# Up projections of a SwiGLU block as seven block products, with the down projections summed in PSUM

## Chip, cores, metric

One NeuronCore of a Trainium2 chip. The metric is the device time of one execution in microseconds, the median of three runs. Five engines run side by side: TensorE (PE; its weight loads are listed as PEld), VectorE (DVE), ScalarE (ACT), GpSimd (POOL) and SyncE (SP), which here issues every transfer.

## What is computed

Two layers of a hybrid block on 512 latent tokens (stream x) and 256 context tokens (stream ctx), width 1024. Layer 1 (the last) runs its second half for x alone. The change touches the tail of each layer:

```python
D_MODEL, SEQ, CTX_LEN, D_FF = 1024, 512, 256, 2816
def residual_tail(x, mix, g1, sh2, sc2, g2, w_out, ln1g, ln1b, w1, w3, w2, ln2g, ln2b):
    x = layer_norm(DEEPNORM_ALPHA * x + g1 * (mix @ w_out), ln1g, ln1b)
    h = x * (1.0 + sc2) + sh2
    ffn = (jax.nn.silu(h @ w1) * (h @ w3)) @ w2
    return layer_norm(DEEPNORM_ALPHA * x + g2 * ffn, ln2g, ln2b)
```

The modulation vectors (sh, sc, g) of a layer are a product of the conditioning with w_mod, 1024 x 6144.

## The kernel before

Everything is fp32. Each operand of a product is split into a rounded part hi and a rest lo (`split`, L168 the cast on ACT, L169 the difference, mostly on DVE), and `mm3` (L172 to L174) adds lo*hi, hi*lo and hi*hi in PSUM, so every product is three matmuls. Weights come through `wload`: a transfer into one of 4 staging buffers (`S4`, L186), then a split into one of 5 pairs (`W8`). Activations lie in 22 buffers `U` and in scratch buffers `FT` (10 in the feed-forward part). PSUM has 4 single banks (`PS`) and 2 double ones (`PD`).

`wout_ffn` does the output projection and the feed-forward part. The 2816 features are 22 tiles of 128. The projection of x runs in two halves of tokens (`wout_mm`), and while the second half is projected, the first is normalised (`res_ln1`, `ln1`, whose last step is L947), transposed and split (`to_hT`, L348, L350). POOL makes the scaled residual of each token tile (`residual`, L954, L955). Then come chunks of 2 feature tiles, the last of 4. For each tile, `upk` multiplies the 8 k-tiles of w1 and of w3 with the activations of a stream (512 tokens of x, 256 of ctx), takes silu on ACT (L1077), the product on DVE (L1078) and splits the result. Then each token tile's part of the down projection is summed over the chunk in a `PD`, multiplied by the gate on DVE (L1154) and added to the residual on POOL (L1155). `ffn_last` does the last chunk, tile by tile, with the LayerNorm behind it; the very last tile goes in quarters of 256 columns.

The program is written in this order, and a scheduler with its own times then orders each engine's queue. Weights are requested in the order of a list (`add`, `getw` with a look-ahead). In layer 0, `fill(2)` puts two steps of the next layer's modulation (`mods`, loads L258, matmuls L272) behind each feature tile: four loads of 512 KB in the same staging buffers.

```python
for k in range(KD):
    mm3(ps[:, :n], w[0][:, k], w[1][:, k], st.hT[k][:, 0, sl], st.hT[k][:, 1, sl], k == 0, k == KD - 1)
```

## Time and profile before

| | us |
|---|---|
| three runs, median (lowest to highest) | 1692.19 (1691.33 to 1692.58) |
| profiled execution, span | 1690.5 |
| PE busy | 1612.5 (95%) |
| DVE, ACT, POOL busy | 919.2, 628.0, 499.4 |
| transfers | 190.82 MB, mean 113 GB/s |

The span runs from the first to the last instruction of one profiled execution; what lies around it (start and end) is in the runs' times and not in the span, 1.7 us by the median. Engine times are sums of instructions, and engines overlap. A matmul's record includes its pipeline, so records of neighbours overlap. The granted clock of PE is given as a share of 2.4 GHz.

### The profile page before, as it was taken

Reading aid. Unit: us, or ns where it says so; the run is one execution under the profiler, and the core shown is the slowest. Engines: PE = TensorE matmul, PEld = TensorE weight load, DVE = VectorE, ACT = ScalarE, POOL = GpSimd, SP = SyncE. Lnnn points to the kernel's source line nnn. Section 1 sums busy time; section 2 is a strip of 40 time slices with the busy share of each in tenths; the row PEclk is TensorE's granted clock in tenths of the full one; section 3 lists DMA queues with packets and bytes.
Section 4 is the critical chain, followed back from the end, with each engine's and each line's share of the span. In section 5 each row is a group of like instructions: output and inputs, shape, how many; then the busy total and the mean of one; then the engine's idle time right before and its main releaser. Section 6 shows DMA issues by size and latency. Waiting matters only on the chain.

```text
span 1690.5 us, 22196 instructions
## 1 busy us (share of the span) xinstructions
PE 1612.5 (95%) x8745; PEld 1339.2 (79%) x8745; DVE 919.2 (54%) x1229; ACT 628.0 (37%) x1113; POOL 499.4 (30%) x412
## 2 busy tenths in 40 slices
PE   6999889999999999999999997989999899999997
PEld 3857778897888887888888876879988788888886
DVE  1434676868843434432444358577859554445455
ACT  2521666875411212121221235457954322212221
POOL 0213011323533133421433015342323432233223
PEclk9999999999999999999999998999999899999999
DMA  9576113135425534453321214411145133222321
GB/s 322 176 223 191 40 39 135 63 108 177 128 64 162 159 103 143 127 167 111 114 64 49 63 51 135 131 57 38 38 161 184 55 97 115 88 87 88 112 99 50
DMA packets 148236, 190.82 MB, mean 113 GB/s; under 512 B 7290, under 2 KB 108268, under 8 KB 148132
## 3 DMA queue, kind: packets, MB, share of 16 engines
q1 hardware_dynamic: 148132, 189.41, 35.2%
q8 instruction: 69, 1.13, 0.3%
q14 instruction: 35, 0.29, 0.1%
HBM read 184.10 MB, written 5.28 MB: 112 GB/s over the span
## 4 chain that ended last, share of the span: by engine, by line
PE 82%; DVE 8%; DMA 3%; ACT 3%; issue 3%; POOL 1%; SPq 0%; POOLq 0%; DVEq 0%; ACTq 0%
PE ps L172 14%; PE ps L174 14%; PE ps L173 14%; PE pd L172 10%; PE pd L173 10%; PE pd L174 10%; PE ps L272 3%; PE ps L719 3%; PE ps L703 2%; DVE u L169 2%; DVE w L169 2%; DMA u<-in_w_mod_dram 1%; ACT u L168 1%; ACT w L168 1%; DMA i<-in_ctx_dram 1%
## 5 line engine op out<-in xcount | busy, mean ns | idle before, releaser
L173 PE MATMUL ps<-u,w 128*128 128x512 f32 (+1 forms) x1216 | 424.5, 349 | 6.7 <-DVE u L169 6.7
L172 PE MATMUL ps<-u,w 128*128 128x512 f32 (+1 forms) x1216 | 423.8, 349 | 1.3 <-DVE modT L298 1.0
L174 PE MATMUL ps<-u,w 128*128 128x512 f32 (+1 forms) x1216 | 423.9, 349 | 0.0
L169 DVE TENSOR_TENSOR w<-s,w 128x1024 fp32r<-128x1024 f32 (+4 forms) x225 | 311.1, 1390 | 193.9 <-ACT w L168 193.0
L168 ACT CAST w<-s 128x1024 fp32r<-128x1024 f32 (+4 forms) x225 | 227.7, 1025 | 506.4 <-PE pd L174 203.4
L1155 POOL TENSOR_TENSOR f<-f,f 128x1024 f32<-128x1024 f32 x90 | 241.4, 2691 | 525.8 <-DVE f L1154 525.8
L172 PE MATMUL pd<-w,u 128*128 128x512 f32 (+5 forms) x824 | 313.2, 380 | 10.5 <-DVE u L169 8.6
L173 PE MATMUL pd<-w,u 128*128 128x512 f32 (+5 forms) x824 | 309.8, 376 | 2.3 <-DVE w L169 2.3
L174 PE MATMUL pd<-w,u 128*128 128x512 f32 (+5 forms) x824 | 307.8, 374 | 0.0
L173 PEld LDWEIGHTS ps<-u,w 128*128 128x128 f32 x1216 | 231.2, 190 | 41.4 <-DVE u L169 7.9
L172 PEld LDWEIGHTS ps<-u,w 128*128 128x128 f32 x1216 | 230.6, 190 | 40.0 <-DVE u L169 3.6
L174 PEld LDWEIGHTS ps<-u,w 128*128 128x128 f32 x1216 | 231.0, 190 | 35.2 <-issue 4.2
L1154 DVE TENSOR_TENSOR f<-pd,f 128x1024 f32<-128x1024 f32 x90 | 110.0, 1222 | 192.3 <-PE pd L174 192.3
L172 PEld LDWEIGHTS pd<-w,u 128*128 128x128 f32 x824 | 156.4, 190 | 52.3 <-DVE u L169 10.8
L173 PEld LDWEIGHTS pd<-w,u 128*128 128x128 f32 x824 | 156.5, 190 | 32.0 <-issue 3.4
L174 PEld LDWEIGHTS pd<-w,u 128*128 128x128 f32 x824 | 156.5, 190 | 29.1 <-issue 1.7
L168 ACT CAST u<-y 128x512 fp32r<-128x512 f32 (+1 forms) x222 | 109.6, 516 | 187.5 <-DVE y L1078 174.0
L169 POOL TENSOR_TENSOR u<-y,u 128x512 fp32r<-128x512 f32 (+1 forms) x60 | 79.0, 1323 | 226.6 <-ACT u L168 204.3
L169 DVE TENSOR_TENSOR u<-y,u 128x256 fp32r<-128x256 f32 (+1 forms) x162 | 107.4, 681 | 50.4 <-ACT u L168 49.7
L1078 DVE TENSOR_TENSOR y<-ps,y 128x512 f32<-128x512 f32 (+1 forms) x70 | 40.2, 574 | 163.4 <-PE ps L174 163.4
L1077 ACT ACTIVATE y<-ps 128x512 f32<-128x512 f32 (+1 forms) x70 | 35.2, 503 | 162.0 <-PE ps L174 161.9
L355 POOL TENSOR_SCALAR st<-st 128x1 f32<-128x1 f32 x30 | 8.3, 277 | 250.6 <-DVE st L1025 125.9
(217 smaller groups left out, 1811.7 us busy)
## 6 DMA issues: line engine op xcount, KB each, us to landing
s<-in_w_ffn_dram SPq DMA_DIRECT2D x132, 512.0 KB
s<-in_w_mod_dram SPq DMA_DIRECT2D x80, 512.0 KB
s<-in_w_out_dram SPq DMA_DIRECT2D x50, 512.0 KB
u<-in_w_mod_dram SPq DMA_DIRECT2D x16, 512.0 KB
s<-in_w_in_dram SPq DMA_DIRECT2D x16, 512.0 KB
s<-in_w_in_dram SPq DMA_DIRECT2D x12, 416.0 KB
...
```

What stands on the lines that cost most here:

```text
L168: A_.copy(out=hi, in_=src)
L169: (eng or V_).tensor_tensor(out=lo, in0=src, in1=f(hi), op=ALU.subtract)
L172: T_.matmul(ps, lhsT=ll, rhs=rh, start=start, stop=False)
L173: T_.matmul(ps, lhsT=lh, rhs=rl, start=False, stop=False)
L174: T_.matmul(ps, lhsT=lh, rhs=rh, start=False, stop=stop)
L272: T_.matmul(ps[32 * j:32 * j + 32, :n], lhsT=sst[:, k, :], rhs=ws[j // 2][:, (j % 2) * n:(j % 2 + 1) * n], start=(k == 0), stop=(k == KD - ...
L703: T_.transpose(pt[:, o:o + P], es[t2][:, k * P:(k + 1) * P], ident)
L719: T_.matmul(av[:, 0:256], lhsT=vt[k][:, h, :], rhs=pts[k // 2][:, a, (k % 2) * 256:(k % 2 + 1) * 256], start=(k == 0 and a == 1), stop=(k ...
L1077: A_.activation(out=y, in_=p1[:, :n], func=AF.Silu)
L1078: V_.tensor_tensor(out=y, in0=p3[:, :n], in1=y, op=ALU.mult)
L1154: V_.tensor_tensor(out=tt, in0=pd.rearrange("p a b -> p (a b)"), in1=gb[st.s], op=ALU.mult)
L1155: G_.tensor_tensor(out=yacc[(st.s, t)], in0=yacc[(st.s, t)], in1=tt, op=ALU.add)
```

## The change

The activations are cut into 2 x 2 blocks: k-tiles 0 to 3 and 4 to 7, and two halves of the tokens, N = 384 each in layer 0 (two x tiles and one ctx tile) and 256 in layer 1. The weights of a feature tile are a 2 x 2 block too: w1 over w3, k-tiles 0 to 3 beside 4 to 7. Of the 22 tiles the first 2 (`NCONV`) are multiplied as before, by token halves; the other 20 take seven block products (Winograd's form) where the plain way has eight. For that

- `up_forms` loads w1 and w3 of a tile into staging and leaves them there until POOL has made four differences and sums of them (L1073, L1074, L1077, L1078, 128x512 each) and ACT and DVE have split seven blocks into three pairs `W8` and one `FT`;
- once a layer, `T1` to `T4`, differences of activation blocks (L1179; 12 on DVE, 4 on POOL), are made and split, 16 pieces;
- `prod` is 4 k-tiles x 3 matmuls (L1186); `finish` completes a tile one iteration later; sums of products in PSUM and SBUF are on DVE (L1218, L1233, L1194), the products with silu on POOL (L1195, L1196);
- the result of each tile is stored to DRAM (`yd`), and the residuals too (`rd`, L1134).

The down projections follow after all 22 tiles: one pass over all features per group of token tiles, two passes of three tiles in layer 0 (w2 is loaded and split twice), one of four in layer 1, summed in PSUM; activations are loaded back and split (`feat`). The gate is multiplied once (in layer 1 into all of w2, L189 of before). `FT` has 14 buffers.

```diff
-        scoped[0] = tc.tile_pool(name=nm(kind), bufs={"inp": 10, "att": 1, "ffn": 10}[kind], reuse_waits="tile")
+        scoped[0] = tc.tile_pool(name=nm(kind), bufs={"inp": 10, "att": 1, "ffn": 14}[kind], reuse_waits="tile")
...
+    NCONV, NLAST = 2, 4
...
+    def up_forms(l, ft):
+        s1, s3 = getw(("1", l, ft), 2), getw(("3", l, ft), 2)
+        lo, hi = slice(0, 512), slice(512, 1024)
+        with tc.high_priority(offset=WOFF):
+            wa = W8()
+            split(wa[:, 0, :D], wa[:, 1, :D], s1)
+            d = Y()
+            G_.tensor_tensor(out=d, in0=s1[:, lo], in1=s3[:, lo], op=ALU.subtract)
+            G_.tensor_tensor(out=s3[:, lo], in0=s3[:, lo], in1=s3[:, hi], op=ALU.add)
+            wb = W8()
+            split(wb[:, 0, :D], wb[:, 1, :D], s3)
+            G_.tensor_tensor(out=s1[:, lo], in0=s3[:, lo], in1=s1[:, lo], op=ALU.subtract)
+            G_.tensor_tensor(out=s1[:, hi], in0=s1[:, hi], in1=s1[:, lo], op=ALU.subtract)
+            wc = W8()
+            split(wc[:, 0, :D], wc[:, 1, :D], s1)
+            wd = FT(F32R, D).rearrange("p (a n) -> p a n", a=2)
+            split(wd[:, 0], wd[:, 1], d)
...
+        for k in range(4):
+            y11, y21, y12, y22 = (Y32[h][k][:, i] for h in range(2) for i in range(2))
+            for e, o, i0, i1, t in ((V_, y11, y12, y11, T1), (G_, y12, y22, y12, T3), (V_, y22, y22, y11, T2),
+                                    (V_, y21, y21, y22, T4)):
+                e.tensor_tensor(out=o, in0=i0, in1=i1, op=ALU.subtract)
+                split(t[k][:, 0], t[k][:, 1], o)
+        B11, B21, B22 = R[0][0:4], R[0][4:8], R[1][4:8]
+
+        def prod(ps, A, B, first, last=False):
+            for k in range(4):
+                for i, (u, v) in enumerate(((1, 0), (0, 1), (0, 0))):
+                    T_.matmul(ps, lhsT=A[u][:, k], rhs=B[k][:, v], start=first and k == 0 and i == 0,
+                              stop=last and k == 3 and i == 2, skip_group_check=True)
+
+        def finish(ft, w, A, Bk, sa, su):
+            prod(A, w["s4"], B22, False, True)
+            A_.activation(out=sa[:, 1], in_=A, func=AF.Silu)
+            prod(Bk, w["a22"], T4, False, True)
+            V_.tensor_tensor(out=su[:, 0], in0=su[:, 0], in1=Bk, op=ALU.add)
+            G_.tensor_tensor(out=sa[:, 1], in0=sa[:, 1], in1=su[:, 1], op=ALU.mult)
+            G_.tensor_tensor(out=sa[:, 0], in0=sa[:, 0], in1=su[:, 0], op=ALU.mult)
...
+            prod(A, w["a11"], B11, True)
+            A_.copy(out=sa[:, 0], in_=A)
+            prod(ps, w["a12"], B21, True, True)
+            V_.tensor_tensor(out=sa[:, 0], in0=sa[:, 0], in1=ps, op=ALU.add)
+            A_.activation(out=sa[:, 0], in_=sa[:, 0], func=AF.Silu)
...
+            if prev:
+                finish(*prev)
...
+            if ft + 1 < NF:
+                wn = up_forms(l, ft + 1)
+            prod(A, w["s2"], T2, False)
+            A_.copy(out=su[:, 0], in_=A)
+            prod(Bk, w["s3"], T3, True)
+            prod(A, w["s1"], T1, False)
+            A_.copy(out=su[:, 1], in_=A)
+            V_.tensor_tensor(out=su[:, 1], in0=su[:, 1], in1=Bk, op=ALU.add)
+            prev = ft, w, A, Bk, sa, su
+            fill(2)
...
+            for ft in range(NF - NLAST):
+                d = nx
+                if ft + 1 < NF - NLAST:
+                    nx = feat(ft + 1)
+                for i in range(len(tiles)):
+                    mm(i, [ft], [d])
```

How the queues change at three places. First POOL in layer 1, from the normalisation of the second token half on (f: scratch, s: a staged weight, y: a difference of weights); before:

```order
L954 TENSOR_TENSOR f_11799<-f_11474,f_11008 128x1024
L954 TENSOR_TENSOR f_11802<-f_11490,f_11008 128x1024
L955 TENSOR_TENSOR f_11799<-f_11799,f_11011 128x1024
L955 TENSOR_TENSOR f_11802<-f_11802,f_11011 128x1024
L1155 TENSOR_TENSOR f_11296<-f_11296,f_11823 128x1024
```

and now:

```order
L966 TENSOR_TENSOR f_11815<-f_11619,f_11143 128x1024
L1179 TENSOR_TENSOR f_11759<-f_11759 128x256
L967 TENSOR_TENSOR f_11811<-f_11811,f_11146 128x1024
L1179 TENSOR_TENSOR f_11760<-f_11760 128x256
L1179 TENSOR_TENSOR f_11761<-f_11761 128x256
L1179 TENSOR_TENSOR f_11762<-f_11762 128x256
L967 TENSOR_TENSOR f_11815<-f_11815,f_11146 128x1024
L1073 TENSOR_TENSOR y_11990<-s_1947_11645,s_1984_11981 128x512
L1073 TENSOR_TENSOR y_12042<-s_1985_11983,s_1986_11985 128x512
L1074 TENSOR_TENSOR s_1984_11981<-s_1984_11981 128x512
L1074 TENSOR_TENSOR s_1986_11985<-s_1986_11985 128x512
L1077 TENSOR_TENSOR s_1947_11645<-s_1984_11981,s_1947_11645 128x512
```

The activation differences and the first weight differences stand behind and between the residual operations, where before only the first additions of the down projection stood.

Second DVE in the middle of layer 1's feature tiles (w: a weight pair, pd and ps: PSUM, u: split activations); before:

```order
L169 TENSOR_TENSOR w_2178_13130<-s_2177_13129,w_2178_13130 128x1024
L1154 TENSOR_TENSOR f_13059<-pd_13058,f_11805 128x1024
L1154 TENSOR_TENSOR f_13075<-pd_13074,f_11805 128x1024
L1154 TENSOR_TENSOR f_13091<-pd_13090,f_11805 128x1024
L1154 TENSOR_TENSOR f_13107<-pd_13106,f_11805 128x1024
L169 TENSOR_TENSOR w_2183_13190<-s_2182_13189,w_2183_13190 128x1024
L1078 TENSOR_TENSOR y_13184<-ps_13135,y_13184 128x512
```

and now:

```order
L169 TENSOR_TENSOR w_2031_12398<-s_2018_12274,w_2031_12398 128x1024
L1218 TENSOR_TENSOR f_12336<-f_12336,ps_12335 128x256
L169 TENSOR_TENSOR f_12412<-y_12401,f_12412 128x512
L1233 TENSOR_TENSOR f_12217<-f_12217,pd_12214 128x256
L169 TENSOR_TENSOR w_2033_12404<-s_2019_12276,w_2033_12404 128x1024
L1233 TENSOR_TENSOR f_12337<-f_12337,pd_12334 128x256
L1194 TENSOR_TENSOR f_12217<-f_12217,pd_12214 128x256
L169 TENSOR_TENSOR w_2034_12409<-s_2018_12274,w_2034_12409 128x1024
L169 TENSOR_TENSOR w_2042_12518<-s_2029_12394,w_2042_12518 128x1024
```

Splits of weights now stand behind sums that wait for a product (L1194), two tiles interleaved.

Third SP in the middle of layer 0's feature tiles, the loads of w1, w3 (128x8x128), w2 and w_mod (128x1024); before, two feature tiles' worth is 14 loads, of which here one tile's:

```order
L186 DMA s_978_5457<-in_w_ffn_dram 128x8x128
L186 DMA s_980_5462<-in_w_ffn_dram 128x8x128
L186 DMA s_997_5566<-in_w_ffn_dram 128x8x128
L186 DMA s_999_5571<-in_w_ffn_dram 128x8x128
L258 DMA s_1010_5703<-in_w_mod_dram 128x1024
L258 DMA s_1011_5705<-in_w_mod_dram 128x1024
L258 DMA s_1013_5712<-in_w_mod_dram 128x1024
```

and now:

```order
L341 DMA s_983_5683<-in_w_ffn_dram 128x8x128
L341 DMA s_984_5685<-in_w_ffn_dram 128x8x128
L260 DMA s_990_5743<-in_w_mod_dram 128x1024
L1199 DMA yd_8_121<-f_5489 128x768
L260 DMA s_991_5745<-in_w_mod_dram 128x1024
L260 DMA s_992_5751<-in_w_mod_dram 128x1024
L260 DMA s_993_5753<-in_w_mod_dram 128x1024
L341 DMA s_998_5819<-in_w_ffn_dram 128x8x128
```

Each tile's two weights and four modulation tiles now follow at once on the next tile's, with the store of a result (yd) among them.

## Rows read from the trace of the kernel before

**Rows 1.** The page's first part: engine, busy us (share of the span) xinstructions.

```profile
PE 1612.5 (95%) x8745; PEld 1339.2 (79%) x8745; DVE 919.2 (54%) x1229; ACT 628.0 (37%) x1113; POOL 499.4 (30%) x412
```

**Rows 2.** Busy time by stretches: us, busy us per engine, PE's granted clock, DMA share, GB/s.

```profile
455.00:470.00 15.00, 11.02 (x74) 10.22 (x73) 10.88 (x7) 5.33 (x12) 9.91 (x4) 0.89 0.20 70
...
505.00:945.00 440.00, 440.00 (x2365) 359.32 (x2365) 172.60 (x185) 85.38 (x117) 133.36 (x50) 1.00 0.38 119
...
1310.00:1330.00 20.00, 14.24 (x66) 11.53 (x65) 13.16 (x14) 6.79 (x17) 11.43 (x8) 0.66 0.03 13
...
1330.00:1640.00 310.00, 310.00 (x1366) 252.15 (x1365) 154.25 (x137) 79.32 (x98) 93.74 (x36) 1.00 0.33 100
```

**Rows 3.** PE in order of time, first and last of two unbroken runs: start, us, operation.

```profile
428.41 0.28 PE L172 MATMUL ps<-u,w 128*128 128x256 f32 x1
...
443.89 0.28 PE L174 MATMUL ps<-u,w 128*128 128x256 f32 x1
...
699.80 0.40 PE L173 MATMUL ps<-u,w 128*128 128x512 f32 x1
...
702.12 0.39 PE L172 MATMUL pd<-w,u 128*128 128x512 f32 x1
```

**Rows 4.** Groups by line and form, weight loads: busy us, mean ns of one, idle before.

```profile
L173 PEld LDWEIGHTS ps<-u,w 128*128 128x128 f32 x1216 | 231.2, 190 | 41.4 <-DVE u L169 7.9 <-issue 2.5
```

**Rows 5.** Groups by line and form, DVE, ACT and POOL.

```profile
L169 DVE TENSOR_TENSOR w<-s,w 128x1024 fp32r<-128x1024 f32 x200 | 281.8, 1417 | 187.0 <-ACT w L168 186.0 <-DMA y<-xn 0.5
...
L1155 POOL TENSOR_TENSOR f<-f,f 128x1024 f32<-128x1024 f32 x90 | 241.4, 2691 | 525.8 <-DVE f L1154 525.8
...
L168 ACT CAST w<-s 128x1024 fp32r<-128x1024 f32 x200 | 207.5, 1049 | 469.0 <-PE pd L174 197.4 <-issue 98.3 <-PE ps L174 71.6
...
L1154 DVE TENSOR_TENSOR f<-pd,f 128x1024 f32<-128x1024 f32 x90 | 110.0, 1222 | 192.3 <-PE pd L174 192.3
...
L1078 DVE TENSOR_TENSOR y<-ps,y 128x256 f32<-128x256 f32 x30 | 12.6, 421 | 47.8 <-PE ps L174 47.8
```

**Rows 6.** Instructions of lines L169 and L1155: minimum/median/maximum ns, first and last start.

```profile
L169 DVE TENSOR_TENSOR w<-s,w x225: 479/1224/3440, 22.4 to 1653.6; 128x1024 fp32r<-128x1024 f32 x101, 128x832 fp32r<-128x832 f32 x6, 128x768 fp32r<-128x768 f32 x2, 128x1032 fp32r<-128x1032 f32 x2
L169 DVE TENSOR_TENSOR u<-y,u x162: 364/425/2627, 25.2 to 1659.5; 128x256 fp32r<-128x256 f32 x106, 128x512 fp32r<-128x512 f32 x56
...
L169 POOL TENSOR_TENSOR u<-y,u x60: 725/1292/2256, 217.2 to 1260.3; 128x512 fp32r<-128x512 f32 x56, 128x256 fp32r<-128x256 f32 x4
...
L1155 POOL TENSOR_TENSOR f<-f,f x90: 2381/2403/3486, 476.9 to 1624.9; 128x1024 f32<-128x1024 f32 x90
```

**Rows 7.** POOL and DVE in order of time, where both work at once.

```profile
345.30 3.52 POOL L169 TENSOR_TENSOR u<-y,u 128x512 fp32r<-128x512 f32 x2 [4.70 <-ACT u L168]
...
345.82 1.85 DVE L169 TENSOR_TENSOR w<-s,w 128x1024 fp32r<-128x1024 f32 x1
...
455.16 4.94 POOL L954 TENSOR_TENSOR f<-f,f 128x1024 f32<-128x1024 f32 x2 [2.34 <-PE ps L348]
460.05 5.02 POOL L955 TENSOR_TENSOR f<-f,f 128x1024 f32<-128x1024 f32 x2
...
456.39 9.30 DVE L169 TENSOR_TENSOR u<-y,u 128x256 fp32r<-128x256 f32 x5 [1.64 <-ACT u L168]
```

**Rows 8.** DVE in order of time: the normalisation of the second token half, both layers.

```profile
441.37 3.89 DVE L947 TENSOR_SCALAR f<-f,st 128x1024 f32<-128x1024 f32 x2 [0.98 <-POOL st L356]
...
1312.01 2.82 DVE L947 TENSOR_SCALAR f<-f,st 128x1024 f32<-128x1024 f32 x1 [0.44 <-POOL st L356]
```

**Rows 9.** Waits of the DMA queue's issues, 480 to 1000: us in total, times, longest us.

```profile
SPq L258 <- DVE w L169: 151.2, 33, 22.4
...
SPq L186 <- PE ps L272: 103.0, 19, 11.4
```

**Rows 10.** The chain that ended last: loads of 512 KB on it (start, us, what).

```profile
419.41 5.21 DMA s<-in_w_ffn_dram
...
1278.42 3.57 DMA s<-in_w_out_dram
```

More of the change, by code (lines that the diff above doesn't have):

```diff
@@ L207, in hybrid_kernel @@
     xc = drp.tile([LC, D], F32, name="xc")
+    rd = [[drp.tile([P, D], F32, name=f"rd{l}_{i}") for i in range(NT)] for l in range(2)]
+    yd = [[drp.tile([P, LJ], F32, name=f"yd{l}_{i}") for i in range(NF)] for l in range(2)]
     bte = [cp.tile([P, 256], F32, name=f"bte{i}") for i in range(2)]
@@ L1064, in wout_ffn, with pieces @@
     def wout_ffn(l, streams, final, hook=None):
-        chunks = ffn_chunks(l)
         X = streams[0]
-        yacc = {}
-        def upk(st, sl, w1, w3, d):
-            n = sl.stop - sl.start
+        both = len(streams) > 1
+        N = 384 if both else 256
+        col = {(0, 0): 0, (0, 1): 128, (0, 2): N, (0, 3): N + 128, (1, 0): 256, (1, 1): N + 256}
+        def pieces(n, src):
+            r = []
+            if both:
+                return [src(F32R, 2 * N).rearrange("p (a b) -> p a b", a=2) for _ in range(n)]
+            for i in range(0, n, 2):
+                t = src(F32R, 4 * N).rearrange("p (k a b) -> p k a b", k=2, a=2)
+                r += [t[:, 0], t[:, 1]]
+            return r[:n]
@@ new lines, in wout_ffn, with half @@
+        R, Y32 = [None, None], [None, None]
+        def half(hv, xt, ct):
+            R[hv] = pieces(KD, U)
+            Y32[hv] = [FT(F32, 2 * N).rearrange("p (a b) -> p a b", a=2) for _ in range(4)]
+            for k in range(KD):
+                ps = PS()
+                for i, t in enumerate(xt + ct):
+                    T_.transpose(ps[:, i * P:(i + 1) * P], t[:, k * P:(k + 1) * P], ident)
+                y = Y32[hv][k % 4][:, k // 4]
+                A_.activation(out=y[:, :256], in_=ps[:, :256], func=AF.Identity, scale=a[:, k:k + 1], bias=b[:, k:k + 1])
+                if ct:
+                    A_.activation(out=y[:, 256:], in_=ps[:, 256:N], func=AF.Identity, scale=ac[:, k:k + 1],
+                                  bias=bcc[:, k:k + 1])
+                split(R[hv][k][:, 0], R[hv][k][:, 1], y)
@@ L1072, in upk, with conv @@
+        def conv(hv, ft, w1, w3):
             p1, p3 = PS(), PS()
@@ L1094, in wout_ffn @@
                 ns.append(n)
-            C.hT = C.alloc(KD)
-            to_hT(ns, lambda k: C.hT[k], *fold2(l, C))
-        to_hT(n0, lambda k: X.hT[k][:, :, 0:256], a, b)
+        half(0, n0, ns[:1])
         for i in range(2):
-            yacc[(0, i)] = residual(n0[i], bc)
+            spool(X, i, n0[i])
+        if both:
+            spool(C, 0, ns[0])
         acc = wout_mm(l, X, 1)
         n1 = [res_ln1(l, X, 2 + i, acc[i], gbc, FT) for i in range(2)]
-        ch = chunks[0]
-        parts = [(X, slice(0, 256))]
@@ L1116, in wout_ffn @@
-        for i in range(2):
-            yacc[(0, 2 + i)] = residual(n1[i], bc)
-        if len(streams) > 1:
-            for i in range(2):
-                yacc[(1, i)] = residual(ns[i], bc)
-        gb = {st.s: gates(l, 1, st.s, FT) for st in streams}
+        for ft in range(NCONV):
+            conv(0, ft, *w13[ft])
+        half(1, n1, ns[1:])
+        for i in range(2):
+            spool(X, 2 + i, n1[i])
+        if both:
+            spool(C, 1, ns[1])
+        for ft in range(NCONV):
+            conv(1, ft, *w13[ft])
```

193 lines of the change are left out of this document (118 added, 75 removed).

## Prediction, made before the change was timed

> **What bounds the kernel now.** Read the page's first part first: TensorE (PE) is busy 1612.5 of 1690.5 us, VectorE (DVE) 54%, ScalarE (ACT) 37%, GpSimd (POOL) 30% [rows 1]. Then the busy time by stretches, for the feed-forward part, which is all that the change touches: in 440 us of layer 0 and 310 us of layer 1 PE is busy for every microsecond at clock 1.00; only where a layer's feed-forward part begins (455 to 470, 1310 to 1330) does it idle, 4.0 and 5.8 us, with a granted clock of 0.89 and 0.66 on average, so partly at the lower level of 1.2 GHz [rows 2]. So there the price of a matmul is its spacing, read from consecutive starts in order of time: from 428.41 to 443.89 there are 132 matmuls of 256 columns, 131 steps of 0.118 us; from 699.80 to 702.12 ten steps of 0.232 us at 512 columns [rows 3]. The records' own durations (0.28 and 0.40 us) overlap and are no price. Spacing is thus nearly proportional to columns; for 384 columns, which the feed-forward part does not have now, I interpolate 0.175 us.
>
> The weight loads decide whether narrower matmuls pay, since the change issues more of them. A load's record lasts 190 ns, longer than a 256-column step of 118 ns, so loads overlap matmuls and cost nothing [rows 3, 4]. The Trainium skill ("TensorE: Matmul & The Clock Gate", Part 3, The mechanism) says that a weight load overlaps matmuls in flight only when the row group differs, and gives about 107 ns for 128 columns (LDWEIGHTS). By that rule the 68 us below would shrink, by an estimate from that page's figures, to some 12; the 118 ns step speaks against it.
>
> **The change, part by part.**
>
> *Columns removed.* Before, a feature tile costs 48 matmuls of 512 and, in layer 0, 48 of 256: 11.1 + 5.7 = 16.8 us in layer 0, 11.15 us in layer 1. Now 20 of 22 tiles take 7 products of 12 matmuls, 84 of 384 (14.7 us) in layer 0, 84 of 256 (9.9 us) in layer 1. Two tiles stay as they were. Saved: 20 x (16.8 - 14.7) + 20 x (11.15 - 9.87) = 42 + 26 = **68 us**. The down projections keep their matmuls: same count, same 512 columns.
>
> *Removed beside PE.* 90 multiplications by the gate (1.22 us on DVE) and 90 additions on POOL (2.69 us) [rows 5]. PE is busy around them, so they give nothing.
>
> *Start of the feed-forward part.* The first seven-product tile needs 16 subtractions of activation blocks and 16 splits of them. In layer 0 the second token half is normalised at 445.3 [rows 8], 16.9 us after the output projection ended [rows 3]. From that end to the first product with a subtracted block PE has two ordinary tiles in two halves (33.6 us), two products (4.2) and transposes (2.6): 40.2 us, so 23 are left at 445.3. POOL has until then 6 residual operations of 2.40 us, 4 subtractions (384 wide, 1.01 by interpolation) and 6 weight differences of 1.29 [rows 6]: 26 us, 1.9 of them begun before. While POOL works, DVE's splits from SBUF are held: four POOL operations of 9.96 us in a row, and five DVE splits, of 0.36 to 0.43 us alone [rows 6], take 9.30 us beside them, one per POOL operation [rows 7]. So some ten DVE operations alternate with POOL's (+5), the last difference comes at 29 us, and a cast (1.05 [rows 5]), the backlog of 14 DVE operations (7) and a split (1.22) follow: 38 us. PE waits 15 us and restarts at a lower clock (2 us more, as after the waits of today). Today's loss there is about 5.5, so **+12 us**, with 0 (the splits pass between) and +25 (each of 36 DVE operations waits) as ends. In layer 1 the same count gives 20 us on POOL, about 29 until the first subtracted product, against 11 us of PE work left at 1314.8 [rows 8]: 18 of waiting and 2 of low clock, less today's 5.8 idle and about 5 at low clock: **+8** (0 to 17).
>
> *The seven products of layer 1.* Each tile now gives POOL four operations of 512 and two of 256 (4 x 1.29 + 2 x 0.73 = 6.6 us, median and minimum of POOL's splits [rows 6]) and DVE three splits of 1024 and one of 512 from SBUF (3 x 1.22 + 0.68 = 4.3 us, the second by interpolation) beside three sums that read PSUM (0.42 each, 1.3 [rows 5]). The sums are not held: the gate multiplication reading PSUM keeps its 1.22 us mean beside POOL, the split from SBUF has 1.42 [rows 5]. Split and POOL exclude each other: a split at 345.82 takes 1.85 us while two POOL operations take 3.52 instead of 2.58 [rows 7]. If the exclusion is complete, a tile needs 10.9 us, over PE's 9.87; if a POOL operation hides 0.28 us of a split (9.96 us where 4 x 2.40 + 4 x 0.37 = 11.1 would be due [rows 6, 7]), 9.2. The Trainium skill ("SBUF — State Buffer", Who interferes with whom) says that the second of the two fully blocks until the first is done. By it the term would be 20 x 1.0 = 20 us. I take 0.6 us a tile, nearer to the full exclusion, since the split weight pairs have five buffers for three per tile: the order of PE leaves a second product's pair two products, 2.8 us, between its buffer and its use, and cast and split alone take 2.3. **+12 us**; ends 0 and +46 (POOL's and all of DVE's work in turn, 12.2 us a tile).
>
> *The seven products of layer 0.* Here a product lasts 2.1 us and the exclusive sum, 7.2 + 4.3, is below 14.7. What is tight is staging: 14 tiles carry four modulation loads each, so six loads of 512 KB go through four buffers in 14.7 + 1.9 us, where two tiles before had 14 in 54 us (2 x 16.8 up, 2 x 8.4 down, 3.7 modulation). Already now SP waits 151 us for DVE's splits and 103 us for the modulation matmuls before it may load [rows 9]. A load lands in 3.6 to 5.2 us [rows 10]: six need 21 to 31 of 66 buffer-microseconds, the two weights are held some 8 us each for their forms, and 5 to 7 us remain for each modulation tile to wait for its turn. That fits, narrowly: **+5 us**, ends 0 and +25 (1.8 us a tile).
>
> *Down projections.* Second loading and splitting of w2 in layer 0, storing and loading of activations, gates folded into all 22 w2 of layer 1: per tile DVE 1.22 + 0.6 us (one more 1.2 in layer 1) and 0.7 MB of loads in 4.2 us or 5.6 us of PE. Covered by PE as long as loads run ahead two tiles. The change of pass in layer 0 finds four of five weight pairs held (about 2 us), and the last token tile is now finished in halves, not quarters (0.8 us): **+3 us** (0 to 8). The queue of SP gets 182 issues more at about 0.4 us, 73 us in all over 800 us of queue: nothing.
>
> *Sum.* -68 + 12 + 8 + 12 + 5 + 3 = -28 us: the profiled span would go from 1690.5 to 1662.5. The runs' median lies 1.7 us above that span, so **1664 us**.
>
> **The rivals.**
>
> *All of it hides.* Splits slip between POOL's operations, and the new work beside PE is covered: only the 3 us of passes and a few of the start stay, 1628. For it: DVE stands at 39 and 50%, POOL at 30% in the two stretches above [rows 2]. Against it: POOL and DVE already wait for each other at the start [rows 7].
>
> *The exclusion of DVE and POOL decides.* One mechanism, three places: both starts at their upper ends (25 + 17) and 12.2 us a tile in layer 1 (46), with 8 for the rest: 96 us against 68, so 1690.5 + 28 + 1.7 = 1720. It turns slower than before once exclusion costs more than 60 us, about double what I book. For it: 12.2 is a plain sum of rows. Against it: POOL's additions and DVE's splits mostly aren't due in the same moment, and PE's order can pair tiles.
>
> *Staging decides in layer 0.* Modulation matmuls stand in PE's order and stop it until their load lands: +25 instead of 5, 1684. For it the waits of SP [rows 9]; against it, the loads are spaced apart on PE.
>
> *Weight loads count.* If a load lay between matmuls, at the 190 ns of its record, 84 matmuls would cost more than 48 in layer 1 (36 x 0.19 = 6.8 us more, against 1.3 saved): 20 x 5.5 = 110 us slower there, and in layer 0 12 loads fewer a tile, 46 us gained: 1690.5 + 110 - 42 - 46 + 40 + 1.7, about 1754 with my other terms. The rule of the Trainium skill named above (Part 3, The mechanism) would bring this about; the spacing of [rows 3] beside the record of [rows 4] all but excludes it.
>
> **How the numbers follow.** 0.2% is 3.4 us, about what a measurement of this kernel can tell from no change. Forecast (1640 to 1690): 0.66. All hides: 0.14. Exclusion decides: 0.12. Staging: 0.07. Weight loads: 0.01. Faster takes forecast, hiding and staging, less the edge: 0.85; slower is exclusion and weight loads: 0.13; the same 0.02. The range takes in most of the hiding case below and the lower part of the exclusion case above: 1630 to 1702.
>
> **What would show it.** Spacing of 0.175 us at 384 columns and 0.118 at 256. PE idle of about 15 us, with a lower clock behind it, at the beginning of both feed-forward parts, released by DVE or ACT splits while POOL is busy without a gap. In layer 1's seven products, PE waits below 1 us a tile, released by splits of weights, and the mean DVE split clearly above 1.42 us. In layer 0 waits for modulation loads below 0.5 us a tile. Wrong would be: waits above 2 us a tile in either layer, or a start without idle time.

## The result and the profile after

The changed kernel takes 1714.8 us (median of 4, 1712.9 to 1717.2) against 1691.8 us of the kernel before on the same chip: ratio 1.0139, 95% interval 1.0125 to 1.0154. The forecast was 1664 us, 1630 to 1702. It is slower by 23 us where 28 less were forecast, so 51 us have to be found.

The page's first part (engine, busy us, share of the span, instructions) answers to [rows 1]:

```profile
PE 1590.8 (93%) x9105; PEld 1363.9 (80%) x9105; DVE 1009.1 (59%) x1361; ACT 771.0 (45%) x1381; POOL 613.7 (36%) x570
```

PE's busy time fell by 22 us, not by 68, and its idle time rose from 78 to 123 us. So two things went wrong: matmuls or their spacing cost more than their columns, and waits came. The stretches tell where. The rows are, as in [rows 2]: us, busy us of PE, PEld, DVE, ACT and POOL with instruction counts, PE's granted clock, DMA share, GB/s. They are layer 0's start, steady products and change to the down projections, then the same three of layer 1.

```profile
425.00:495.00 70.00, 47.76 (x261) 45.96 (x262) 60.21 (x71) 28.14 (x56) 36.54 (x24) 0.85 0.33 108
540.00:740.00 200.00, 198.98 (x1040) 157.56 (x1039) 76.32 (x94) 62.16 (x96) 91.12 (x65) 1.00 0.59 181
820.00:865.00 45.00, 39.78 (x190) 35.35 (x190) 25.05 (x34) 23.11 (x39) 7.43 (x6) 0.96 0.71 219
1303.00:1350.00 47.00, 33.40 (x230) 30.87 (x228) 45.16 (x63) 20.38 (x46) 23.42 (x18) 0.86 0.34 114
1364.00:1540.00 176.00, 164.12 (x1343) 159.61 (x1342) 105.78 (x112) 82.93 (x143) 132.47 (x98) 1.00 0.42 128
1540.00:1600.00 60.00, 48.70 (x296) 43.58 (x295) 43.51 (x48) 25.80 (x45) 16.90 (x12) 0.91 0.64 203
```

Five of the six have idle time of PE, 5 to 22 us each. The mean granted clock of 0.85, 0.86 and 0.91 in three of them says that PE runs partly at 1.2 GHz after its waits. The second stretch has 1.0 us of idle time, and still it holds too little: 1040 matmuls in 200 us. What PE does there, in order of time (start, us, operation, count):

```profile
603.46 1.05 PE L274 MATMUL ps<-s,sst 128*32 128x512 f32 x4
604.44 0.98 PE L1186 MATMUL pd<-u,w 128*128 128x384 f32 x4
605.25 1.21 PE L1186 MATMUL pd<-f,w 128*128 128x384 f32 x6
606.39 1.05 PE L274 MATMUL ps<-s,sst 128*32 128x512 f32 x4
607.38 1.83 PE L1186 MATMUL ps<-u,w 128*128 128x384 f32 x9
```

L274 are the modulation matmuls (L272 before). The same view of the kernel before, where they stand:

```profile
505.04 1.92 PE L272 MATMUL ps<-s,sst 128*32 128x512 f32 x16
506.90 0.50 PE L172 MATMUL ps<-u,w 128*128 128x512 f32 x1
```

Before, 16 records take 1.86 us to the next matmul, 0.116 each. Now 4 records take 0.98 us, 0.245 each. The program gives a modulation step four matmuls on four column groups of 32; two read one loaded vector, two the other. Each matmul leaves two records, one after the other, so the 24 steps are 192 records, and a quartet is four records side by side. Before, all four matmuls stand in a row, and in the trace four records start within 0.02 us. Now each pair waits for a load of its own and has products between it and the other pair, so only two run at once: 44 of the 46 groups in the trace are such a pair, with its four records, where before there were 12 groups of two whole steps.

For a full account I took, from 400 us on, every step from one matmul's start to the next and subtracted its columns by the spacing of [rows 3] (0.175 us at 384, confirmed: 17 steps take 2.97 us from 425.11 on). What is left is waiting, low clock and restarts, by which the longer steps into and out of a group of modulation matmuls are meant; these matmuls themselves are counted by their steps alone. The columns come to 69 to 71 us, by how the spacing is rounded.

| Term | booked, us | measured, us |
|---|---|---|
| columns | -68 | -70.7 |
| start, layer 0 | +12 | +20.3 (8.1 to 28.4) |
| start, layer 1 | +8 | +10.4 (12.7 to 23.1) |
| steady products, layer 1 | +12 | +21.1 (0 to 21.1) |
| steady products, layer 0, with the modulation | +5 | +32.3 (matmuls 22.3 to 46.0, waits and restarts 2.8 to 11.4) |
| change to the down projections, passes, end | +3 | +21.2 (7.6 in layer 0, 13.0 in layer 1, 0.6) |
| change from layer 0 to 1, work before the start | 0 | -10.7 |
| sum | -28 | +23.9 (spans: +23.2) |

PE's longest sums in the view of waits (line that waits, releaser, us in total, times, longest us), in 425 to 496, 1302 to 1364, 1364 to 1540 and 1541 to 1600:

```profile
PE pd L1186 <- DVE w L169: 18.2, 1, 18.2
...
PE pd L1186 <- DVE w L169: 6.4, 1, 6.4
...
PE pd L1186 <- ACT f L1232: 9.4, 8, 1.3
...
PE pd L1186 <- DVE w L169: 5.7, 1, 5.7
```

At both starts and at layer 1's change to the down projections it is a split of weights (DVE L169). In layer 1's steady products it is a copy out of PSUM on ACT, which looks harmless. One such wait, ACT and then PE in order of time:

```profile
1444.04 2.00 ACT L168 CAST w<-s 128x1024 fp32r<-128x1024 f32 x2 [1.81 <-POOL s L1078]
...
1446.73 0.37 ACT L1232 COPY f<-pd 128x256 f32<-128x256 f32 x1
...
1447.19 1.66 PE L1186 MATMUL pd<-u,w 128*128 128x256 f32 x12 [1.12 <-ACT f L1232]
```

The copy stands on ACT behind casts that waited 1.81 us for a weight difference on POOL (L1078). So the releaser that PE names is two steps away from the engine that is late.

POOL and DVE at the start of layer 0, in order of time, answer to [rows 7]:

```profile
452.28 4.90 POOL L1179 TENSOR_TENSOR f<-f 128x384 f32<-128x384 f32 x4
457.15 2.70 POOL L967 TENSOR_TENSOR f<-f,f 128x1024 f32<-128x1024 f32 x1
459.81 2.70 POOL L966 TENSOR_TENSOR f<-f,f 128x1024 f32<-128x1024 f32 x1
...
452.31 10.61 DVE L169 TENSOR_TENSOR u<-f,u 128x384 fp32r<-128x384 f32 x6 [2.25 <-ACT u L168]
462.85 3.69 DVE L1179 TENSOR_TENSOR f<-f,f 128x384 f32<-128x384 f32 x3
...
473.55 1.46 POOL L1078 TENSOR_TENSOR s<-s 128x512 f32<-128x512 f32 x1
...
479.09 0.55 DVE L169 TENSOR_TENSOR u<-f,u 128x384 fp32r<-128x384 f32 x1
...
488.99 2.29 PE L1186 MATMUL pd<-u,w 128*128 128x384 f32 x6 [18.25 <-DVE w L169]
```

Six splits take 10.6 us beside six POOL operations; later, with POOL idle, one takes 0.55. That is the exclusion that the prediction describes. But POOL's last operation there ends at 475.0 us and PE starts again at 489.0: for 14 of its 18.2 us PE waits while POOL is idle and VectorE works off what has piled up. In layer 1 POOL's last operation ends at 1339.2, and PE starts again at 1350.1.

### The profile page after: what moved, and what is told of

The parts are those of the page before. It is cut to its first block, busy times and chain, and to the rows that moved or that the text cites. A ratio compares the mean times of both kernels' runs of the same rounds, so it can differ in the third digit from the quotient of the medians.

```text
span 1713.7 us, 24043 instructions
## 1 busy us (share of the span) xinstructions
PE 1590.8 (93%) x9105; PEld 1363.9 (80%) x9105; DVE 1009.1 (59%) x1361; ACT 771.0 (45%) x1381; POOL 613.7 (36%) x570
## 4 chain that ended last, share of the span: by engine, by line
PE 69%; DVE 13%; DMA 5%; ACT 5%; issue 4%; POOL 3%; SPq 1%; DVEq 0%; POOLq 0%; ACTq 0%
PE pd L1186 18%; PE pd L172 9%; PE pd L173 9%; PE pd L174 9%; PE ps L274 4%; PE ps L172 4%; DVE u L169 4%; PE ps L174 4%; PE ps L173 4%; DVE w L169 3%; PE ps L731 3%; PE ps L1186 3%; PE ps L715 2%; ACT w L168 2%; DMA s<-in_w_ffn_dram 2%
## 5 line engine op out<-in xcount | busy, mean ns | idle before, releaser
L169 DVE TENSOR_TENSOR w<-s,w 128x1024 fp32r<-128x1024 f32 (+2 forms) x287 | 391.5, 1371 | 283.9 <-ACT w L168 282.0
L168 ACT CAST w<-s 128x1024 fp32r<-128x1024 f32 (+2 forms) x287 | 293.8, 1030 | 477.0 <-PE pd L1186 116.7
L1186 PE MATMUL pd<-u,w 128*128 128x256 f32 (+1 forms) x2040 | 320.6, 310 | 46.7 <-DVE w L169 30.3
L1186 PEld LDWEIGHTS pd<-u,w 128*128 128x128 f32 x2040 | 296.8, 191 | 76.6 <-DVE w L169 31.1
L172 PE MATMUL pd<-w,u 128*128 128x512 f32 (+5 forms) x728 | 276.2, 380 | 12.3 <-DVE u L169 6.4
L173 PE MATMUL pd<-w,u 128*128 128x512 f32 (+5 forms) x728 | 273.3, 376 | 1.9 <-DVE w L169 1.9
L174 PE MATMUL pd<-w,u 128*128 128x512 f32 (+5 forms) x728 | 271.6, 374 | 0.0
L169 POOL TENSOR_TENSOR u<-y,u 128x512 fp32r<-128x512 f32 (+1 forms) x60 | 78.8, 1321 | 226.4 <-ACT u L168 204.2
L168 ACT CAST u<-y 128x512 fp32r<-128x512 f32 (+2 forms) x178 | 94.6, 545 | 56.0 <-PE pd L1186 20.9
L1077 POOL TENSOR_TENSOR s<-s,s 128x512 f32<-128x512 f32 x40 | 67.0, 1676 | 135.9 <-DVE w L169 81.4
L169 DVE TENSOR_TENSOR u<-y,u 128x512 fp32r<-128x512 f32 (+2 forms) x118 | 74.5, 642 | 48.5 <-ACT u L168 47.7
L1195 POOL TENSOR_TENSOR f<-f,f 128x384 f32<-128x384 f32 (+1 forms) x40 | 60.8, 1521 | 70.9 <-ACT f L1192 70.9
L1073 POOL TENSOR_TENSOR y<-s,s 128x512 f32<-128x512 f32 x40 | 56.6, 1417 | 75.2 <-DMA s<-in_w_ffn_dram 68.8
L169 DVE TENSOR_TENSOR u<-ps,u 128x512 fp32r<-128x512 f32 (+2 forms) x106 | 67.1, 655 | 27.0 <-ACT u L168 25.8
L172 PE MATMUL ps<-w,u 128*128 128x512 f32 (+1 forms) x208 | 80.8, 395 | 1.1 <-ACT w L168 1.1
L173 PE MATMUL ps<-u,w 128*128 128x256 f32 (+2 forms) x224 | 76.0, 341 | 6.3 <-DVE u L169 6.3
L173 PE MATMUL ps<-w,u 128*128 128x512 f32 (+1 forms) x208 | 81.3, 392 | 0.0
L174 PE MATMUL ps<-w,u 128*128 128x512 f32 (+1 forms) x208 | 81.0, 391 | 0.0
```

Source lines behind the costliest of these rows:

```text
L168: A_.copy(out=hi, in_=src)
L169: (eng or V_).tensor_tensor(out=lo, in0=src, in1=f(hi), op=ALU.subtract)
L172: T_.matmul(ps, lhsT=ll, rhs=rh, start=start, stop=False)
L173: T_.matmul(ps, lhsT=lh, rhs=rl, start=False, stop=False)
L174: T_.matmul(ps, lhsT=lh, rhs=rh, start=False, stop=stop)
L1073: G_.tensor_tensor(out=d, in0=s1[:, lo], in1=s3[:, lo], op=ALU.subtract)
```

## The experiments

Each time is the median of that kernel's executions, each ratio is against the kernel before, executed beside it (1691.7 to 1694.2 us in the different groups), so differences of 2 or 3 us between experiments are not read. "Lost" is PE time by the account above, and "the changes" are those from products to down projections, one in each layer. Layer 0's steady figures stand as modulation matmuls plus the rest.

### Modulation quartets behind one load

```diff
+ w = S4(4 * n)
+ nc.sync.dma_start(out=w..., in_=src[k, :, types[0]:types[0] + 2, c0:c0 + 2 * n])
- filler += [mods(1, (0, 1), 0, 512), ...]
+ filler += [mods(1, ty, c, 256, one=True) for ty in (...) for c in (0, 512)]
...
- fill(2)
+ fill(4)
```

> Against the changed kernel (1714.8 us): one modulation load now brings both vectors, 256 columns each way, so all four matmuls that share one pass of TensorE wait for the same load; loads and bytes stay the same. Theory 'cut quartets' (layer 0's modulation matmuls cost 46 us instead of 22 because the pairs of a quartet stand apart in PE's order, with about 5 us of slow restarts): 18 to 25 us faster, modulation matmuls about 24 us in all. Rival 'staging' (products wait for loads and buffers): within 3 us of 1714.8, with the time back as waits for loads.

1704.7 us, ratio 1.0076 (1.0061 to 1.0091): 10 us faster, half of what 'cut quartets' expected. The modulation matmuls fell, from 46.0 to 30.6 us (24 were expected); eight records of 256 columns, a step of half the width, take 0.57 us:

```profile
602.93 0.64 PE L279 MATMUL ps<-s,sst 128*32 128x256 f32 x8
603.50 2.37 PE L1191 MATMUL pd<-u,f 128*128 128x384 f32 x12
```

But waits and restarts in the steady products rose from 11.4 to 18.7 us. PE's waits in 500 to 820, where the changed kernel had 1.0 us for these loads:

```profile
PE ps L279 <- DMA s<-in_w_mod_dram: 8.7, 9, 2.6
```

So the cut quartets are real, and with them gone part of the time comes back as waits for loads, the rival's mechanism.

### Weight forms on VectorE

```diff
- G_.tensor_tensor(out=d, in0=s1[:, lo], in1=s3[:, lo], op=ALU.subtract)
+ V_.tensor_tensor(out=d, in0=s1[:, lo], in1=s3[:, lo], op=ALU.subtract)
```

and so the other three of `up_forms`.

> The four weight sums and differences of each seven-product tile move from GpSimd to VectorE. Theory 'exclusion' (GpSimd and VectorE hold each other up): waits of layer 1's steady products fall from 20 to under 8 us, both starts shorten by 3 to 6 us; 1695 to 1702. Rival 'VectorE is full' (60% busy there, 2.7 us more per tile): the waits grow, 1720 or more. Rival 'order' (waits come from where the splits stand in the order): within 4 us of 1714.8.

1700.2 us, ratio 1.0051 (1.0036 to 1.0066), 15 us faster. Layer 1's steady products lose 7.7 instead of 21.1 us. The same stretch, windows and PE's waits:

```profile
1364.00:1540.00 176.00, 173.56 (x1429) 169.75 (x1428) 140.99 (x190) 93.00 (x158) 42.59 (x35) 1.00 0.48 147
```

```profile
PE pd L1186 <- DVE f L1233: 1.5, 1, 1.5
PE pd L1186 <- ACT f L1229: 0.5, 1, 0.5
```

VectorE is busy 80% instead of 60% of that stretch, and PE's listed waits there fall from 11.4 to 2.0 us. 'VectorE is full' is out. The starts did not both get shorter: layer 0's loses 25.0 instead of 28.4 us, layer 1's 25.8 instead of 23.1, where 3 to 6 us less were expected of both.

### Copies out of ACT's queue

```diff
- A_.copy(out=su[:, 0], in_=A)
+ V_.tensor_copy(su[:, 0], A)
- A_.copy(out=su[:, 1], in_=A)
+ V_.tensor_copy(su[:, 1], A)
```

> The changed kernel (1714.8 us) with the two PSUM copies of each seven-product tile on VectorE instead of ScalarE, where they stood behind casts that wait for GpSimd's forms. Theory 'pace' (GpSimd and VectorE's work from SBUF, in turn, need about 11 us a tile against TensorE's 9.9): layer 1's steady waits stay at 13 to 20 us, released by another instruction; 1711 to 1720. Rival 'queue' (only the copies' place behind the casts stops TensorE): the waits fall under 7 us, 1700 to 1707.

1725.7 us, ratio 1.0194 (1.0171 to 1.0217): 11 us slower than the changed kernel, beyond what 'pace' named. The waits of layer 1's steady products grew from 16.8 to 25.0 us and changed their releaser to DVE, so the place behind the casts alone is not the cause; the move also gave VectorE two operations more a tile. 17.2 tiles took 191.3 us in the changed kernel, 11.1 each; here 11.6, with the forms on VectorE 10.4. By starts and durations, POOL or a DVE operation without PSUM was at work in 93% of 1364 to 1540 (POOL 75%, DVE 51%). That the shared pace sets the time is borne out by both runs; they don't separate the exclusion from POOL's own slowness (1.29 us for a form, 0.68 on VectorE). The records of that stretch show both: a weight split takes 1.45 us on average, 1.22 in the run with the forms on VectorE, and a form of L1077 takes 1.83 us.

### Raw rows to DRAM

```diff
- y = residual(n, bc)
- nc.sync.dma_start(out=rd[l][st.jt + t], in_=y)
+ nc.sync.dma_start(out=rd[l][st.jt + t], in_=n)
...
  nc.sync.dma_start(out=y, in_=rd[l][st.jt + t])
+ G_.tensor_tensor(out=y, in0=y, in1=bc[0], op=ALU.mult)
+ G_.tensor_tensor(out=y, in0=y, in1=bc[1], op=ALU.add)
```

The scale and shift vectors `bc` are now fetched ahead of the down pass, no longer ahead of the output projection.

> The normalised rows are stored as they are and get their scale and shift on GpSimd after the reload, in the down pass, where GpSimd idles; 20 operations of 2.4 to 2.7 us leave the start of the feed-forward parts. Theory 'exclusion': PE's waits at the start of layer 0 fall from 24 to 10 to 14 us, in layer 1 from 15 to 8 to 11; 1698 to 1707. Rival 'order' (casts and splits of the first weights stand behind the activation splits on ScalarE and VectorE): within 3 us of 1714.8.

1710.5 us, ratio 1.0111 (1.0095 to 1.0126), 4 us faster, outside both expectations. The starts did what 'exclusion' said, layer 0's from 28.4 to 18.0 us and layer 1's from 23.1 to 17.7. But both changes got dearer, from 7.6 to 12.3 and from 13.0 to 18.8 us: the time moved to the next place, where these operations and the fetch of `bc` now stand.

### Priority of the forms

```diff
- with tc.high_priority(offset=WOFF):
+ with tc.high_priority(offset=300):
```

in `up_forms`.

> The weight forms get a priority 300 instead of 100 instructions ahead in the order. Theory 'order': at the change from products to down projections the last forms no longer stand behind splits for the down pass, and at the start not behind activation splits: 10 to 20 us faster. Rival 'buffers' (forms wait for staging buffers and split weights, whatever the order): within 4 us, or slower since activation splits come later.

1715.0 us, ratio 1.0133 (1.0116 to 1.0150). Nothing, as 'buffers' said; the run does not tell which resource it is.

### All differences off GpSimd

The two edits above (forms on VectorE, raw rows) and:

```diff
- (G_, y12, y22, y12, T3)
+ (V_, y12, y22, y12, T3)
```

> Three moves together: weight forms on VectorE, rows stored raw, and all sixteen activation differences on VectorE, so that GpSimd has nothing at the start but what the normalisation needs. Theory 'exclusion': the gains add, 14 us in layer 1's steady products, 10 to 14 at the start of layer 0, 4 to 8 in layer 1: 1684 to 1692. Rival 'serial VectorE' (what is left at the start is VectorE's and ScalarE's own work in a row, and moving more to VectorE gives it back): the start of layer 0 stays at 14 us of waits or more, 1692 to 1700.

1689.1 us, ratio 0.9983 (0.9971 to 0.9995). Layer 0's start loses 13.1 us, with 9.5 of waits, layer 1's 15.8, its steady products 6.1. The time lies in the range of 'exclusion', and layer 0's waits are under the 14 us that 'serial VectorE' named. Starts and products give 38 us together; the run is only 26 us faster, mostly because the changes now lose 11.8 and 19.0.

### Down weights fetched later

```diff
- s1, s3 = getw(("1", l, ft), 2), getw(("3", l, ft), 2)
+ la = 2 if ft < NF - 1 else 0
+ s1, s3 = getw(("1", l, ft), max(la, 1)), getw(("3", l, ft), la)
```

on the changed kernel.

> The first two blocks of the down projection's weights are no longer fetched ahead of the last tile's forms. Theory 'pairs' (at the change two of the five split-weight buffers are taken by blocks that nothing can use yet, so the last forms go one by one): waits at the change fall from 6 to 3 us in layer 0 and from 9 to 3 to 5 in layer 1, 7 to 12 us in all with the clock. Rival 'late loads' (the wait moves to the first down block): within 3 us of 1714.8.

1709.4 us (1704.5 to 1710.0), ratio 1.0095 (1.0077 to 1.0113): 5.4 us faster by the medians, between the two expectations. In the profiled execution, the fastest of the four, layer 1's change loses 2.3 instead of 13.0 us, layer 0's 8.3 instead of 7.6. PE's waits in 1541 to 1600:

```profile
PE pd L1187 <- DVE w L169: 2.2, 1, 2.2
PE pd L1187 <- DVE f L1234: 1.8, 1, 1.8
PE pd L1187 <- ACT f L1193: 1.2, 1, 1.2
```

So in layer 1 a good part of the loss is that blocks of w2, which nothing can use yet, are fetched ahead of the last forms and hold split-weight buffers. In layer 0 it is something else, and that stays open.

### Modulation at the start

20 of the 48 steps ahead of the first product, on the quartet kernel:

```diff
+ fill(20)
  for ft in range(NCONV, NF):
...
- fill(4)
+ fill(2)
```

> Quartets as in the run with one load for both vectors, and 20 of the 48 steps stand at the start of layer 0's products, where TensorE waits some 20 us anyway. Theory 'idle at the start is free': the 20 steps cost nothing there, 8 to 13 us faster than the quartet run (1704.7): 1692 to 1697. Rival 'they block': TensorE takes them in order and their loads and buffers delay the first forms, 1703 to 1712.

1726.8 us, ratio 1.0203 (1.0186 to 1.0220), slower than either expectation. TensorE takes its queue in order and stood in front of each load, in 428 to 559:

```profile
PE ps L279 <- DMA s<-in_w_mod_dram: 41.1, 15, 18.3
```

### The parts together

Forms and differences on VectorE, raw rows, quartets, later fetch of w2:

> Weight forms and differences on VectorE, raw rows, quartets, late fetch of the down weights. If the causes are separate and add: 1714.8 less 10 (quartets), 14 (forms), 12 to 18 (starts), 7 to 12 (change): 1661 to 1672. If they share one bottleneck (VectorE or staging): 1680 to 1692.

1666.8 us, ratio 0.9848 (0.9834 to 0.9863): the causes add. The gains of the three runs above (25.7, 10.1 and 5.4 us) sum to 41, and together they give 48. What is left over the columns: starts 13.1 and 17.4 us, steady products 29.6 + 10.7 and 5.8, changes 10.4 and 14.8.

Then the scale and shift vectors fetched in the fourth block of the down pass:

```diff
- bc = lnbc("ln1_g", l, ALPHA), lnbc("ln1_b", l, ALPHA)
+ bc = None
...
+ if ft == 4 and bc is None:
+     bc = lnbc("ln1_g", l, ALPHA), lnbc("ln1_b", l, ALPHA)
```

> The combined kernel, with the scale and shift vectors for the raw rows fetched four blocks into the down pass instead of ahead of its first loads. Theory 'queue' (storing raw rows made the change from products to down projections 5 us longer in each layer because these two transfers wait for a free buffer and hold the queue behind them): 6 to 10 us faster than the combined kernel, 1657 to 1661. Rival 'something else in the change': 1664 to 1668.

1664.9 us, ratio 0.9833 (0.9813 to 0.9853): within the rival's range, so the queue is not it. What holds TensorE up can be read in this kernel's layer 1, POOL, DVE and PE in order of time:

```profile
1526.47 6.20 POOL L1301 TENSOR_TENSOR f<-f,u 128x1024 f32<-128x1024 f32 x2
1532.64 6.08 POOL L1302 TENSOR_TENSOR f<-f,u 128x1024 f32<-128x1024 f32 x2
...
1524.50 2.56 DVE L169 TENSOR_TENSOR u<-y,u 128x512 fp32r<-128x512 f32 x1
1526.99 3.42 DVE L189 TENSOR_TENSOR s<-s,f 128x1024 f32<-128x1024 f32 x1
1530.33 2.90 DVE L169 TENSOR_TENSOR u<-y,u 128x512 fp32r<-128x512 f32 x1
...
1540.99 0.80 PE L173 MATMUL ps<-w,u 128*128 128x512 f32 x1 [7.41 <-DVE w L169]
```

The moved residual (L1301, L1302) runs on POOL without a gap; a split that takes 0.69 us in that pass takes 2.56 and 2.90, the multiplication by the gate 3.42 instead of 1.22, and PE waits 7.4 us for a split.

On top of it, the priority of the forms, the modulation in the down passes (fill(2) there, none in the products), and six staging buffers (the scratch pool 12 instead of 14):

> As the run before, with the weight forms 300 instructions ahead in the order. Alone, on the changed kernel, that priority gave nothing (1715.0). Theory 'forms last' (with GpSimd out of the way, TensorE's remaining waits of 7 and 8 us at the two starts are for weight forms that stand behind activation splits on VectorE): 5 to 12 us faster than the run before. Rival 'buffers' (the forms wait for split-weight buffers that the two ordinary tiles still hold): within 3 us.

1666.8 us, ratio 0.9853 (0.9828 to 0.9877): nothing again, as the rival said.

> As the first run of this group, with the 48 modulation steps moved from layer 0's products to its down projections, two to a block. Theory 'staging' (their loads compete with the products' weights for four buffers): layer 0's products lose their remaining waits and the steps stand closer together, 3 to 8 us faster than that run. Rival 'they cost the same anywhere' (27 us of TensorE and 5 of slow restarts): within 3 us. Third: the down projections, which need a weight block every 4.2 us, start to wait for loads: slower by 5 us or more.

1690.3 us, ratio 0.9985 (0.9971 to 0.9999): 25 us slower, the third case. The steady products of layer 0 got rid of 37 us (290.2 to 252.9 us for the same 252 us of columns, so a product part without modulation loses hardly anything). But in the down projections the matmuls of the modulation take 41 us by their steps, and PE waits there; 786 to 1000:

```profile
PE pd L172 <- DVE u L169: 9.9, 4, 5.3
PE ps L279 <- DMA s<-in_w_mod_dram: 6.4, 4, 3.4
```

> As the first run of this group, with six staging buffers instead of four (the scratch pool gives up two of fourteen). Theory 'staging' (raw weights that stay for their forms make loads late): modulation steps and the change of both layers get faster, 4 to 10 us in all. Rival 'split-weight buffers or the vector engines' bound the change: within 3 us.

1674.7 us, ratio 0.9890 (0.9870 to 0.9909): slower by 10, outside both expectations. Layer 0's steady products get 14.7 us of waits. The scratch pool is smaller too, and it is the likelier cause: the run with six split-weight buffers below has the same smaller pool, but four staging buffers, and shows waits of the same kind in the same place (7.3 us before products in 740 to 806), while with fourteen scratch buffers (the run with late vectors) PE's listed waits in 487 to 800 are 2.3 us, all for modulation loads. A run with the pool alone changed was not made.

### The residual on VectorE

```diff
- if ft == 6:
-     for st, t in tiles:
+ if ft in (6, 8, 10, 12) and len(ya) < len(tiles):
+     st, t = tiles[len(ya)]
...
- G_.tensor_tensor(out=y, in0=y, in1=bc[0], op=ALU.mult)
- G_.tensor_tensor(out=y, in0=y, in1=bc[1], op=ALU.add)
+ V_.tensor_tensor(out=y, in0=y, in1=bc[0], op=ALU.mult)
+ V_.tensor_tensor(out=y, in0=y, in1=bc[1], op=ALU.add)
```

> The combined kernel with late scale vectors (1664.9 us); the scale and shift of the raw rows, in the down pass, move from GpSimd to VectorE, one row tile every second block. Theory 'exclusion, once more' (GpSimd's eight operations in a row hold up VectorE's gating and splits; TensorE waits 7.4 us there in layer 1): 6 to 9 us faster, 1656 to 1659. Rival 'the last forms' (the wait comes from the last tile's forms and the late weight loads): within 2 us.

1653.0 us, ratio 0.9763 (0.9745 to 0.9781): 12 us faster than the kernel that it changes (1664.9 us), more than the 6 to 9 expected, the best of all and 2.4% faster than the kernel before. The edit does two things, it moves the operations and it spreads them over four blocks; which of them gives how much was not tried. Its stretches, in the order of those of the changed kernel above:

```profile
424.00:494.00 70.00, 62.06 (x361) 58.57 (x360) 50.40 (x85) 33.27 (x64) 2.21 (x6) 0.93 0.30 94
540.00:740.00 200.00, 197.35 (x1259) 174.20 (x1258) 108.12 (x155) 68.77 (x106) 33.97 (x27) 1.00 0.61 181
786.00:831.00 45.00, 41.57 (x202) 37.42 (x201) 30.84 (x40) 25.65 (x40) 6.29 (x5) 0.96 0.81 258
1268.00:1316.00 48.00, 39.00 (x297) 37.41 (x296) 38.86 (x78) 24.12 (x52) 1.83 (x4) 0.89 0.37 111
1322.00:1498.00 176.00, 174.17 (x1435) 170.39 (x1435) 142.57 (x189) 93.19 (x157) 42.45 (x35) 1.00 0.47 145
1498.00:1550.00 52.00, 48.21 (x261) 41.54 (x260) 48.31 (x55) 24.71 (x38) 8.98 (x5) 0.97 0.72 238
```

POOL is near idle at both starts, and VectorE, with more to do, is busy for less time there than in the changed kernel (50 instead of 60 us, 39 instead of 45).

### What is left at the starts

One ordinary tile (NCONV = 1), and six split-weight buffers (scratch pool 12), both on that kernel:

> As the run before, with one ordinary tile instead of two: 3.4 us of columns less, two of five split-weight buffers less in use at the starts, and 8.4 and 5.6 us less work of TensorE that covers the start. Theory 'buffers': the waits for the first forms shrink, 3 to 10 us faster. Rival 'VectorE's row of work' (differences, splits and forms take as long as before): the waits grow by what cover is lost, 10 to 20 us slower.

> As the first run of this group, with six split-weight buffers instead of five (the scratch pool gives up two of fourteen). Theory 'buffers': the waits of 7 and 8 us for the first forms fall to 3 to 5, 4 to 9 us faster. Rival 'VectorE's row of work': within 2 us, or slower since the scratch pool is smaller.

1669.3 us, ratio 0.9855 (0.9839 to 0.9872), and 1666.2 us, ratio 0.9838 (0.9814 to 0.9863), 16 and 13 us slower than that kernel. PE's wait for the first forms, layer 0 and layer 1, with one ordinary tile:

```profile
PE pd L1190 <- DVE w L169: 15.4, 1, 15.4
...
PE pd L1190 <- DVE w L169: 13.4, 1, 13.4
```

With two tiles it was 7.1 and 8.4. It grows by 8.3 and 5.0 us, about the cover that was taken away (8.4 and 5.6), and with six buffers it stays 7.1 and 8.4 (the loss of that run is in the steady products, 19.5 and 12.8 us over columns and modulation; the scratch pool is smaller there). So both runs speak for the rival: what is left at the starts is VectorE's own row of differences, splits and forms.

## Why the prediction was wrong

**The columns** were right: 0.175 us at 384 columns, 70.7 us saved against 68. The weight loads cost nothing: 0.175 us is under the 190 ns of a load's record. The prediction quotes half of a rule: the same section of the Trainium skill ("TensorE: Matmul & The Clock Gate", Part 3, The mechanism) lets a load pass matmuls in flight also when it goes to the background weight buffer, and the spacing agrees with that. By the half that is quoted the 68 us would shrink to about 17, not 12, an estimate from that page's 107 ns (36 loads more a tile in layer 1, 12 fewer in layer 0, 20 tiles each).

**The step that failed** is "That fits, narrowly: +5 us, ends 0 and +25". It measured +32. The step asked whether loads arrive in time, and they do: PE's waits for them are 1.0 us in 540 to 740. What it took as given was the "1.9 us" of the modulation matmuls, their old price. Now the two halves of a step wait for two loads and have products between them, and work that ran four at a time runs two at a time. The quartet run shows 15 us of it directly (46.0 to 30.6): with one load for both halves they stand together. That the four busy staging buffers are why the two loads come apart is argued and not tried by itself. Another 8 are what 48 steps of half the width cost one by one, over the 22.3 us of groups of two whole steps. The other 9 are the restarts: the steps into and out of a group of modulation matmuls are longer than their columns by 0.2 us together, 46 times instead of 12 (10.9 instead of 2.5 us, 1.0 of it waits for loads). Without modulation in the products the combined kernel loses 1.5 us there, with it 11. The Trainium skill ("TensorEngine Tiling (Array Packing)", Tiling Modes, Key Properties) says that tiles work in parallel and that a change of the tiling mode drains TensorE. The traces agree with both: in the trace of before the last quartet of a group takes 0.52 us to the next matmul where those ahead of it took 0.41 to 0.43, and in the trace of the change the first product behind it 0.28 instead of 0.175. The order of PE, which needs no measurement, already has the pairs apart; the prediction went by the orders of POOL, DVE and SP alone. (Its "14 tiles" are 12, 24 steps at two a tile; that would only have lowered the term.)

**"Down projections ... +3 us (0 to 8)"** measured +21. I priced the change of pass in layer 0, and not the change from products to down projections, where the look-ahead of the last tile fetches w2 into split-weight buffers that the last forms need. Fetching later gives back 10.7 us of it in layer 1 in the profiled execution, 5.4 by the medians. Layer 0's 7.6 us are not explained; PE's waits in it are 2.5 us for a sum out of PSUM (DVE L1233) and 2.2 for a cast of the first w2 (ACT L168).

**"I take 0.6 us a tile"** measured 1.2 (21.1 us, 17.2 tiles). The place is as forecast, and the mechanism fits; the size is that of the full sum, 10.9 us a tile computed, 11.1 measured. The choice of the middle had no row behind it. PE's releaser was forecast as weight splits and was ACT's copies, which stand behind casts that wait for POOL.

**The starts** were right in kind: +20 (forecast 12, end 25) and +10 (8, end 17; its own terms sum to 9), waits released by weight splits. In layer 0 POOL was done where the forecast had it (475.0 us; forecast 29 us after 445.3), but VectorE then needed 14 us to the last split that PE waits for, and not 9. Taking POOL's work away gives 15 us back in layer 0 and 7 in layer 1; what stays is VectorE's.

**The rival "exclusion decides"** gave 1720, near the result, but not by its sum: it had 88 us at the starts and in layer 1, where 52 were measured, and 8 for the rest, where 54 came. "All of it hides" was out at each start. "Staging decides in layer 0" had the place right and the mechanism wrong: it had the modulation matmuls as waits for loads, which were 1.0 us, and not at a price of their own. No case had that price or the change to the down projections in it, so 0.13 for slower was too little: the starts of layers 0 and 1, the steady products of layer 1 and the staging of layer 0 all got the middle of their ranges or less, and all missed to the same side. The signs could not have told: neither sign of being wrong came, and the waits for modulation loads and those of layer 1 (16.8 us over 17.2 tiles) stayed under their limits, as forecast.

**The gain not booked**, 10.7 us, lies mostly where layer 0 hands over to layer 1: PE's waits in 990 to 1065 were 16.3 us and are 9.9. Which of the edits did that was not tried.
